# The last two output blocks of a diffusion layer: GpSimd's additions move to VectorE, ScalarE's products are added in one wide operation

## The chip, the cores and the metric

The kernel runs on one core of a Trainium2 chip. A core has engines with their own instruction queues: TensorE (PE, matmuls; weight loads are shown as PEld), VectorE (DVE), ScalarE (ACT) and GpSimd (POOL) for arithmetic, and SyncE (SP), which here only issues transfers. Transfers between the main memory and the on-chip memory SBUF are also issued from ScalarE's and GpSimd's queues; all run on the same 16 DMA engines. TensorE writes its results to PSUM, which GpSimd does not read in this program. Engines meet through semaphores only.

The metric is the device time of one execution in microseconds (us).

## What is computed

One layer of a hybrid diffusion backbone on 384 tokens (128 context tokens, 256 latent tokens) of width 2048, all in float32. What matters here is the end of the layer, the second half of the feed-forward part:

```
ff = (silu(h @ w_ffn_gate) * (h @ w_ffn_up)) @ w_ffn_down
x  = x + ga2 * rmsnorm(ff, norm_post_ffn)
```

with

```
rmsnorm(x, g) = x * rsqrt(mean(x * x, axis=-1) + 1e-6) * g
```

`ga2` is a gate for each channel, one for context and one for latent tokens. The output is `x`, transposed: channels on the 128 partitions, tokens along the row.

## The kernel before

The kernel holds activations transposed (16 blocks of 128 channels by 384 tokens) and streams all weights from the main memory. Each weight is split into a high and a low part, and each product is made of three matmuls of the parts. That fills nearly all of the time; the change stands behind it, in the last 15 us, where the down projection of the last hidden chunk ends and the result is normalised, gated, added to `x` and stored. The order of instructions there is the order in which the code issues them, on all five engines (`manual_schedule`, L1897): no scheduler moves anything, and only waits delay it.

The 384 tokens are three tiles `t` of 128 (tile 0 context, tiles 1 and 2 latent). For each tile the sum over chunks lies in SBUF with tokens on partitions, as four units `unit(t, n)` of 512 channels (L1551). For a tile the end goes:

- `last_products` (L1911): TensorE's last matmuls into the banks `pdn`. `add_last` (L1820): VectorE adds a bank to its unit, ScalarE sums the squares.
- `most`, `factor`, `inverse` (L1921 to L1932): the factor `r = 1 / sqrt(mean + eps)` of each token.
- `scale` (L1934): a unit times `r`, on VectorE or ScalarE, 512 wide.
- `turn` (L1944): TensorE transposes four 128x128 pieces of a unit into a PSUM tile `py[t, q]`. Where the unit isn't scaled, it multiplies by `dg` instead of the identity: `dg` is the identity times `r` (L2011), so that transposing and scaling are one matmul.
- `final(t, k)` (L1955): the gate `mods[:, 5, k]` (with the norm's weight folded in) times the piece, plus `x`, into `x1b`, which holds `x` and then the output. Either VectorE does both in one operation out of PSUM (L1964), or ScalarE makes the product into a scratch tile `ep` (L1961) and GpSimd adds it (L1962). `finals(t, q, on_act)` does the four pieces of unit `q`.
- `store` (L1966): one transfer of four pieces, 256 KB, from SyncE's queue or, where named, ScalarE's.

In tile 0 and tile 1 unit 1 goes over ScalarE and GpSimd. At the very end also unit 3 of tile 1 and unit 3 of tile 2 do:

```
finals(1, 3, True)
for q in (0, 1, 3, 2):
    turn(2, q, dg if q in (0, 2) else None)
store(12, 16, 1, 2)
finals(2, 3, True)
```

So GpSimd makes 16 additions of 128x128 here, four for each of these units, and two of the last five stores wait for it. After the last store every engine runs into the closing line of the program (L2093; L2097 in the changed kernel): SyncE waits for all output transfers, each engine drains, and all meet.

Of the kernel before, what the change touches and what calls it, by code (L numbers as in the profile page):

```python
# [20 lines left out]
P = 128  # L21
# [86 lines left out]
def tile_step(ctx: ExitStack, tc: tile.TileContext, a, o):  # L108
    nc = tc.nc
    PE, ACT, DVE, POOL, SP = nc.tensor, nc.scalar, nc.vector, nc.gpsimd, nc.sync  # L110
# [21 lines left out]
    mods = const.tile([P, 6, KT, 2], F32, name="mods")  # L132
# [886 lines left out]
    with ExitStack() as s:  # L1019
# [64 lines left out]
        for kb in range(0, KT, 4):  # L1084
            for x_ in range(2):
                for k in range(kb, kb + 4):
                    q = 32 * (k % 4)
# [9 lines left out]
    with ExitStack() as s:  # L1097
# [166 lines left out]
        for b, i in mix_order:  # L1264
# [18 lines left out]
            else:  # L1283
# [10 lines left out]
                p = psm.tile([P, T], F32, tag="mm", name="pmm")  # L1294
# [19 lines left out]
    with ExitStack() as s:  # L1314
# [5 lines left out]
        ep = [pe.tile([P, 512], F32, name=f"ep{n}", bufs=1) for n in range(6)]  # L1320
# [43 lines left out]
        for i in range(KT):  # L1364
            p = psm.tile([P, T], F32, tag="mm", name="pmm")
# [185 lines left out]
        def unit(t, n):  # L1551

            return psums[n // 2][:, 3 * (n % 2) + t, :]
# [192 lines left out]
        for u in range(HEAD):  # L1746
            kind, c, j = ffn_order[u]
            dst_of[kind](hp[u], c, j)
        n = 0
        for kind, c, j in ffn_order[HEAD:]:  # L1750
            p = psm.tile([P, T], F32, tag="mm", name="pmm")
# [82 lines left out]
        pd_tiles, hid_last, x1b, done = None, None, None, 0  # L1834
        for kind, c, i in steps[:-4]:
            last_c = c == NFC - 1 and kind == "D"
            if last_c and hid_last is not None and x1b is None:
                while pend:
                    pend.pop(0)()
                x1b = actp.tile([P, KT, T], F32, tag="A_hi", name="x1b")  # L1840
# [77 lines left out]
        def col(x, t):  # L1918
            return x[:, t : t + 1]
# [14 lines left out]
        def scale(eng, t, n):  # L1934
            f = unit(t, n)
            if eng is ACT:
                ACT.mul(f, f, col(r3, t))
            else:
                eng.tensor_scalar_mul(f, f, col(r3, t))

        py = {}
        py_pools = {0: [pss] * 4, 1: [psm] * 3 + [pss], 2: [pss] * 4}

        def turn(t, q, diag=None):  # L1944

            pool = py_pools[t][q]
            py[t, q] = pool.tile([P, 4, P], F32, tag="side" if pool is pss else "mm", name="py")
            for j in range(4):
                src = unit(t, q)[:, j * P : (j + 1) * P]
                if diag is None:  # L1950
                    PE.transpose(py[t, q][:, j, :], src, ident)
                else:
                    PE.matmul(py[t, q][:, j, :], src, diag, start=True, stop=True)

        def final(t, k, on_act=False):  # L1955

            src, dst = py[t, k // 4][:, k % 4, :], x1b[:, k, t * P : (t + 1) * P]
            m = mods[:, 5, k, min(t, 1) : min(t, 1) + 1]
            if on_act:
                tmp = ep[1 + k % 5][:, t * P : (t + 1) * P]  # L1960
                ACT.mul(tmp, src, m)  # L1961
                POOL.tensor_add(dst, dst, tmp)  # L1962
            else:
                DVE.scalar_tensor_tensor(dst, src, m, dst, op0=ALU.mult, op1=ALU.add)  # L1964

        def store(k0, k1, t0, t1, eng=SP):  # L1966
            cs = slice(t0 * P, t1 * P)
            eng.dma_start(o["yT"][:, k0:k1, cs], x1b[:, k0:k1, cs])
# [9 lines left out]
        def finals(t, q, on_act=False):  # L1978
            for k in range(4 * q, 4 * q + 4):
                final(t, k, on_act)  # L1980
# [29 lines left out]
        inverse(2)  # L2010
        DVE.tensor_scalar_mul(dg, ident, col(r3, 2))  # L2011
        scale(ACT, 2, 3)
        scale(DVE, 2, 1)
        finals(1, 3, True)
        for q in (0, 1, 3, 2):
            turn(2, q, dg if q in (0, 2) else None)
        store(12, 16, 1, 2)
        finals(2, 3, True)
        finals(2, 0)
        store(0, 4, 2, 3)  # L2020
        finals(2, 1)
        store(4, 8, 2, 3)
        finals(2, 2)
        store(12, 16, 2, 3)
        store(8, 12, 2, 3, ACT)

# [1 line left out]
def _tiles(w, n=P):  # L2028
# [74 lines left out]
```

## Time and profile before

| what | value |
|---|---|
| time, median of 3 runs | 1940.2 us (1939.46 to 1941.09) |
| span of the profiled execution, first to last instruction | 1937.5 us |
| TensorE busy | 1916.2 us (99%) |
| VectorE busy | 1650.8 us (85%) |
| ScalarE busy | 915.3 us (47%) |
| GpSimd busy | 85.8 us (4%) |
| additions of `final` on GpSimd (L1962) | 16, 456 ns each |

The profile is of one execution; what it gives of that execution's length is the span alone. "Busy" leaves out what the sequencers do by themselves (waits, drains, issuing transfers). In the groups of instructions a row reads: line, engine, operation, written tile <- read tiles, partitions x elements, count, then busy time, the mean of one, the idle time before them and who ended it. In the timeline a row begins with start and length in us, and instructions of one line that follow each other are merged.

### The profile page before, as it was taken

How to read it: one execution, taken by the hardware profiler on the slowest of the kernel's cores; microseconds unless marked ns; L12 is line 12 of the kernel's file. 1: busy time of each engine (PE TensorE's matmuls, PEld its weight loads, DVE VectorE, ACT ScalarE, POOL GpSimd, SP SyncE). 2: the span in 40 equal slices, each digit the busy share in tenths (PEclk: the TensorE clock that was granted, in tenths of full speed). 3: DMA queues.
4: the chain of work that ended last, by engine and by line, in shares of the span. 5: the costliest groups of instructions: out<-in, count | busy, mean ns of one | idle time of the engine just before them, and what ended most of it. 6: DMA issues, size and time to landing. Idle time of an engine off the chain costs nothing.

```text
span 1937.5 us, 27470 instructions
## 1 busy us (share of the span) xinstructions
PE 1916.2 (99%) x10494; PEld 1689.0 (87%) x10494; DVE 1650.8 (85%) x2168; ACT 915.3 (47%) x1301; POOL 85.8 (4%) x154
## 2 busy tenths in 40 slices
PE   8999999999999999999999999999999999999997
PEld 5679999999999999999988888888888888888886
DVE  5559897889969898978789888999998999988885
ACT  4235455545456654456454444444444443444444
POOL 0001111100000000104000000000000000000001
PEclk9999999999999999999999999999999999999999
DMA  9976766766757886655263636362636272625243
GB/s 389 392 280 229 259 232 224 255 227 198 223 170 244 303 287 208 233 196 196 89 198 126 199 107 196 115 214 95 218 102 217 88 223 92 201 76 185 87 174 110
DMA packets 200904, 380.53 MB, mean 196 GB/s; under 512 B 14228, under 2 KB 126964, under 8 KB 196420
## 3 DMA queue, kind: packets, MB, share of 16 engines
q1 hardware_dynamic: 181540, 320.84, 48.8%
q0 software_dynamic: 13952, 50.39, 8.4%
q10 hardware_dynamic: 5280, 7.55, 1.1%
q8 instruction: 82, 1.34, 0.3%
q14 instruction: 50, 0.41, 0.1%
HBM read 361.94 MB, written 16.78 MB: 195 GB/s over the span
## 4 chain that ended last, share of the span: by engine, by line
PE 92%; DMA 3%; DVE 3%; ACT 1%; issue 0%; SPq 0%; DVEq 0%; ACTq 0%
PE pgu L338 31%; PE pmm L326 31%; PE pdn L338 18%; PE pv L491 3%; DMA slab<-in_w_ada 2%; PE pfo L1043 1%; PE pf L1243 1%; PE pgm L474 1%; PE pmm L1520 1%; PE ptr L1812 1%; PE pfo L1044 1%; PE pf L1244 1%; PE po L788 1%; DVE wlo L287 0%; DMA raw<-in_w_br_gla 0%
## 5 line engine op out<-in xcount | busy, mean ns | idle before, releaser
L326 PE MATMUL pmm<-A_hi,whi 128*128 128x384 f32 x1088 | 366.9, 337 | 0.0
L326 PE MATMUL pmm<-A_lo,whi 128*128 128x384 f32 x1088 | 364.1, 335 | 0.3 <-DVE A_lo L379 0.3
L326 PE MATMUL pmm<-A_hi,wlo 128*128 128x384 f32 x1088 | 364.2, 335 | 0.0
L1667 ACT CAST whi<-u 128x1024 fp32r<-128x1024 f32 x200 | 210.7, 1053 | 271.9 <-DVE u L1651 86.2
L1667 ACT CAST whi<-raw 128x1024 fp32r<-128x1024 f32 x175 | 184.1, 1052 | 211.9 <-DMA raw<-in_w_g 73.6
L1678 DVE TENSOR_TENSOR wlo<-u,whi 128x1024 fp32r<-128x1024 f32 x200 | 244.2, 1221 | 28.0 <-ACT whi L1667 16.8
L338 PE MATMUL pgu<-whi,A_hi 128*128 128x512 f32 x640 | 250.0, 391 | 0.0
L338 PE MATMUL pgu<-whi,A_lo 128*128 128x512 f32 x640 | 249.3, 389 | 0.0
L1678 DVE TENSOR_TENSOR wlo<-raw,whi 128x1024 fp32r<-128x1024 f32 x175 | 213.5, 1220 | 34.2 <-ACT whi L1667 24.6
L287 DVE TENSOR_TENSOR wlo<-raw,whi 128x1024 fp32r<-128x1024 f32 x165 | 200.8, 1220 | 32.4 <-ACT whi L300 32.1
L300 ACT CAST whi<-raw 128x1024 fp32r<-128x1024 f32 x151 | 158.0, 1049 | 125.5 <-DMA raw<-in_w_out 46.5
L707 DVE SCALAR_TENSOR_TENSOR adacc<-adaw,spad,adacc 128x1024 f32<-128x1024 f32 x170 | 210.4, 1279 | 3.3 <-DMA adaw<-in_w_ada 3.1
L326 PEld LDWEIGHTS pmm<-A_hi,whi 128*128 128x128 f32 x1088 | 204.2, 188 | 3.3 <-issue 1.7
L326 PEld LDWEIGHTS pmm<-A_lo,whi 128*128 128x128 f32 x1088 | 204.4, 188 | 1.0 <-DVE A_lo L379 0.8
L326 PEld LDWEIGHTS pmm<-A_hi,wlo 128*128 128x128 f32 x1088 | 204.2, 188 | 0.4 <-DVE wlo L287 0.2
L338 PE MATMUL pdn<-whi,hid_hi 128*128 128x512 f32 x480 | 186.9, 389 | 0.0
L338 PE MATMUL pdn<-whi,hid_lo 128*128 128x512 f32 x480 | 186.8, 389 | 0.0
L338 PE MATMUL pgu<-wlo,A_hi 128*128 128x512 f32 x640 | 184.2, 389 | 0.0
L338 PEld LDWEIGHTS pgu<-whi,A_hi 128*128 128x128 f32 x640 | 120.1, 188 | 26.1 <-issue 0.8
L338 PEld LDWEIGHTS pgu<-wlo,A_hi 128*128 128x128 f32 x640 | 120.1, 188 | 25.4
L338 PEld LDWEIGHTS pgu<-whi,A_lo 128*128 128x128 f32 x640 | 120.1, 188 | 25.0
L338 PE MATMUL pgu<-whi,S 128*128 128x512 f32 x480 | 131.1, 395 | 0.0
(398 smaller groups left out, 2998.4 us busy)
## 6 DMA issues: line engine op xcount, KB each, us to landing
adaw<-in_w_ada POOLq DMA_DIRECT2D x96, 512.0 KB, 3.9
raw<-in_w_d SPq DMA_DIRECT2D x88, 512.0 KB, 4.0
slab<-in_w_ada SPq DMA_DIRECT2D x32, 1024.0 KB, 10.3
raw<-in_w_gate SPq DMA_DIRECT2D x64, 512.0 KB, 4.3
raw<-in_w_g SPq DMA_DIRECT2D x48, 512.0 KB, 3.8
raw<-in_w_u SPq DMA_DIRECT2D x48, 512.0 KB, 3.8
raw<-in_w_in SPq DMA_DIRECT2D x46, 512.0 KB, 4.5
u<-in_w_u SPq DMA_DIRECT2D x40, 512.0 KB, 4.6
```

Of the source, the lines that this page charges most:

```text
L287: eng.tensor_sub(lo, raw, hi.bitcast(F32))
L300: ACT.copy(hi, raw)
L326: PE.matmul(dst, w[wi][:, k * n + n0 : k * n + n0 + P], x[xi][:, k0 + k, :], start=first and k == 0 and j == 0, stop=last and k == kts - 1 ...
L338: PE.matmul(dst, stat[x_][m], mov(w[w_], m), start=first and w_ == m == x_ == 0, stop=last and w_ == m == 1,)
L474: PE.matmul(pgv[q : q + 32, :], spad[:, k, :], slab[k // (KT // 2)][:, k % (KT // 2), :], start=k < 4, stop=k >= KT - 4,)
L491: PE.matmul(pv[2 * t + g], hT[x_][:, kb, t * P : (t + 1) * P], w_[:, g * 512 : (g + 1) * 512], start=kb == 0 and j == 0, stop=kb == KT - 1 ...
L707: DVE.scalar_tensor_tensor(acc[:, c, :], w, spad[:, k, c : c + 1], acc[:, c, :], op0=ALU.mult, op1=ALU.add,)
L788: PE.matmul(dst, w[wi], x[xi], start=first and j == 0, stop=last and j == 2)
L1043: PE.matmul(p, w_of[0][:, i, k, g, :], x[:, :, lo:hi], start=kt == 0, stop=False)
L1044: PE.matmul(p[:, 0], w_of[1][:, i, k, g, :], x[:, 0, lo:hi], start=False, stop=kt == KT - 1)
L1667: ACT.copy(hi, src)
L1678: DVE.tensor_sub(lo, src, hi.bitcast(F32))
```

## The change

GpSimd's additions for unit 3 of tile 1 and unit 3 of tile 2 go. Unit 3 of tile 1 takes the way over VectorE alone. Unit 1 of tile 2 is scaled by ScalarE instead of VectorE. TensorE transposes unit 3 of tile 2 ahead of units 1 and 2. ScalarE still makes the four products of that unit, but into the four quarters of one scratch tile `ep[4]`, and VectorE adds that tile to `x1b` in one operation of 128x4x128, between the blocks of units 1 and 2. The store of that unit moves from SyncE's queue to ScalarE's, and that of unit 2, now the last, to SyncE's.

```diff
         inverse(2)
         DVE.tensor_scalar_mul(dg, ident, col(r3, 2))
         scale(ACT, 2, 3)
-        scale(DVE, 2, 1)
-        finals(1, 3, True)
-        for q in (0, 1, 3, 2):
+        scale(ACT, 2, 1)
+        finals(1, 3)
+        for q in (0, 3, 1, 2):
             turn(2, q, dg if q in (0, 2) else None)
         store(12, 16, 1, 2)
-        finals(2, 3, True)
+        wide = ep[4].rearrange("p (j x) -> p j x", j=4)
+        for k in range(12, 16):
+            ACT.mul(wide[:, k - 12, :], py[2, 3][:, k - 12, :], mods[:, 5, k, 1:2])
         finals(2, 0)
         store(0, 4, 2, 3)
         finals(2, 1)
         store(4, 8, 2, 3)
+        last = x1b[:, 12:16, 2 * P : 3 * P]
+        DVE.tensor_add(last, last, wide)
+        store(12, 16, 2, 3, ACT)
         finals(2, 2)
-        store(12, 16, 2, 3)
-        store(8, 12, 2, 3, ACT)
+        store(8, 12, 2, 3)
```

GpSimd's queue, its last rows. `x1b` is the output tile, `ep` the scratch tiles with ScalarE's products (the numbers tell them apart). Before:

```order
L1962 TENSOR_TENSOR x1b<-x1b,ep_7649 128x128
L1962 TENSOR_TENSOR x1b<-x1b,ep_7651 128x128
L1962 TENSOR_TENSOR x1b<-x1b,ep_7647 128x128
L1962 TENSOR_TENSOR x1b<-x1b,ep_7648 128x128
L1962 TENSOR_TENSOR x1b<-x1b,ep_7649 128x128 x2
L1962 TENSOR_TENSOR x1b<-x1b,ep_7650 128x128
L1962 TENSOR_TENSOR x1b<-x1b,ep_7651 128x128
L1962 TENSOR_TENSOR x1b<-x1b,ep_7647 128x128
L1962 TENSOR_TENSOR x1b<-x1b,ep_7649 128x128
L1962 TENSOR_TENSOR x1b<-x1b,ep_7650 128x128
L1962 TENSOR_TENSOR x1b<-x1b,ep_7651 128x128
L1962 TENSOR_TENSOR x1b<-x1b,ep_7647 128x128
```

and now:

```order
L1962 TENSOR_TENSOR x1b<-x1b,ep_7649 128x128
L1962 TENSOR_TENSOR x1b<-x1b,ep_7651 128x128
L1962 TENSOR_TENSOR x1b<-x1b,ep_7647 128x128
L1962 TENSOR_TENSOR x1b<-x1b,ep_7648 128x128
L1962 TENSOR_TENSOR x1b<-x1b,ep_7649 128x128
L2097 UNCONDITIONAL_BRANCH
```

Both begin with the last addition of tile 0; the four behind it are unit 1 of tile 1 (before, the row with x2 holds its last one and the first of the next unit). The eight of the two last units are gone, and the branch to the closing line follows at once.

VectorE's queue from tile 2's factor on (`r` the factor, L2011 the scaled identity `dg`, `psums` the units, L1964 the blocks of `final`, `py` the transposed units), the difference of the two:

```order
 L1932 RECIPROCAL r_9635<-r_9635 128x1
 L2011 TENSOR_SCALAR ep_7646<-ident,r_9635 128x128
-L1939 TENSOR_SCALAR psums<-psums,r_9635 128x512
 L1964 SCALAR_TENSOR_TENSOR x1b<-py,mods,x1b 128x128 x12
-L2093 UNCONDITIONAL_BRANCH
+L2026 TENSOR_TENSOR x1b<-x1b,ep_7650 128x4x128
+L1964 SCALAR_TENSOR_TENSOR x1b<-py,mods,x1b 128x128 x4
+L2097 UNCONDITIONAL_BRANCH
```

The scaling is gone. The twelve operations of L1964 were units 0, 1 and 2 of tile 2; now the first four of them are unit 3 of tile 1, and the wide addition (L2026) stands ahead of the last four.

ScalarE's queue in the same place (L1929 is tile 2's factor, L1937 the scaling of a unit, L1961 and L2020 the products, L1968 the store). Before:

```order
L1929 ACTIVATE r_9635<-ssq,bias_16826 128x1
L1937 ACTIVATE psums<-psums,r_9635 128x512
L1961 ACTIVATE ep_7649<-py,mods 128x128
L1961 ACTIVATE ep_7650<-py,mods 128x128
L1961 ACTIVATE ep_7651<-py,mods 128x128
L1961 ACTIVATE ep_7647<-py,mods 128x128
```

and now:

```order
L1929 ACTIVATE r_9635<-ssq,bias_16826 128x1
L1937 ACTIVATE psums<-psums,r_9635 128x512 x2
L2020 ACTIVATE ep_7650<-py,mods 128x128 x4
L1968 DMA out_yT<-x1b 128x4x128
L2097 UNCONDITIONAL_BRANCH
```

The four products shown before are those of unit 3 of tile 1; they are gone and a second scaling stands in their place. The four products of unit 3 of tile 2 all go to one tile now, and the store behind them is that of unit 3 instead of unit 2.

## The prediction

> **What bounds the kernel now.** I read the page first, then the chain of waits at its end.
>
> ```profile
> span 1937.5 us, 27470 instructions
> ...
> PE 92%; DMA 3%; DVE 3%; ACT 1%; issue 0%; SPq 0%; DVEq 0%; ACTq 0%
> ```
>
> ```profile
> 1923.82 0.30 DVE ep L2011
> 1924.11 0.14 issue
> 1924.25 1.14 PE py L1953 x8
> ...
> 1927.58 1.03 DVE x1b L1964 x4
> ```
>
> TensorE carries 92% of the chain, and the change touches none of that: only the last 14 us can move. The second fence is that end (start, duration, what). The chain view stops at VectorE's last operation, 1927.58 + 1.03 = 1928.61, yet the span runs to 1937.5. The missing 8.9 us hold only sequencer work, so I asked for the rows of the kernel's closing line, L2093 (the end of the program), and of its opening, L2085 (durations min/median/max in ns, then first and last start).
>
> ```profile
> L2093 POOLq DRAIN  x3: 46/102/9207, 1927.5 to 1937.2; - x3
> L2093 SPq DRAIN  x3: 7/7/7, 1932.7 to 1936.9; - x3
> ...
> L2093 DVEq DRAIN  x2: 19/739/1459, 1927.2 to 1937.0; - x2
> L2093 ACTq DRAIN  x2: 8/80/153, 1929.1 to 1936.9; - x2
> ```
>
> ```profile
> L2085 POOLq DRAIN  x1: 182/182/182, 0.3 to 0.3; - x1
> ```
>
> ```profile
> SPq L2093 <- PEq L2093: 4.5, 2, 4.1
> SPq L2093 <- DMA out_yT<-x1b: 3.3, 4, 1.2
> ```
>
> Each engine ends in a DRAIN, which is over when the engine is empty, and then all meet. GpSimd's first one starts at 1927.5 and takes 9.207 us, to 1936.7; the closing exchange brings the span to 1937.5, so that exchange is 0.8 us. Everyone else is done much earlier: SyncE, which waits for the output transfers, drains at 1932.7 and then idles 4.1 us (third fence: us in all, times, longest; the engine named there, PE, has long been done, and the only work still open is GpSimd's). So the end is **set by GpSimd's drain**, 4 us behind the last transfer.
>
> ```profile
> 1921.19 1.70 POOL L1962 TENSOR_TENSOR x1b<-x1b,ep 128x128 f32<-128x128 f32 x4 [2.24 <-ACT ep L1961]
> 1924.87 1.69 POOL L1962 TENSOR_TENSOR x1b<-x1b,ep 128x128 f32<-128x128 f32 x4 [1.99 <-ACT ep L1961]
> 1926.73 1.69 POOL L1962 TENSOR_TENSOR x1b<-x1b,ep 128x128 f32<-128x128 f32 x4 [0.17 <-ACT ep L1961]
> ```
>
> GpSimd's last addition ends at 1926.73 + 1.69 = 1928.42, so the drain lasts 8.3 us beyond it. VectorE's drain ends 0.05 us after its last operation (1927.2 + 1.459 = 1928.66), ScalarE's takes 0.15 us: only GpSimd's outlasts its work.
>
> The Trainium skill, "Perfetto Trace Analysis", section "Per-engine timelines", says that of a sequencer-only instruction such as DRAIN the profiler reports the execution alone, and the wait for semaphores lies before it. By that the 9.207 us are GpSimd's own work; were they a wait for the transfers, the gain would be that of the second rival below.
>
> ```profile
> L691 POOL DMA_DIRECT2D adaw<-in_w_ada x96 | 51.0, 531 | 751.9 <-DVE adacc L707 457.1 <-DVE vr L379 132.5 <-DVE adacc L705 78.8
> ...
> L1012 POOL DMA_DIRECT2D wr<-in_w_br_four x4 | 2.3, 582 | 0.3 <-POOL wr L1007 0.3
> ```
>
> One thing sets this drain apart from the 0.182 us one at the start: between them GpSimd issued 100 transfers. Neither kernel differs there, so I take 8.3 us behind the last addition as a constant.
>
> **The other end: the transfers.** All output goes out in stores of 256 KB.
>
> ```profile
> 1926.59 2.29 SPq L1968 DMA_DIRECT2D out_yT<-x1b  x4
> ...
> 1928.64 0.40 ACTq L1968 DMA_DIRECT2D out_yT<-x1b  x1
> ```
>
> ```profile
> out_yT<-x1b SPq DMA_DIRECT2D x1, 256.0 KB, 2.3
> ```
>
> ```profile
> out_yT<-x1b ACTq DMA_DIRECT2D x1, 256.0 KB, 4.0
> ```
>
> ```profile
> 1928.00:1930.00 2.00, 0.00 (x0) 0.00 (x0) 0.61 (x3) 0.00 (x0) 0.42 (x2) 0.79 1.01 281
> 1930.00:1932.00 2.00, 0.00 (x0) 0.00 (x0) 0.00 (x0) 0.00 (x0) 0.00 (x0) 0.50 0.99 291
> ...
> 1933.00:1936.00 3.00, 0.00 (x0) 0.00 (x0) 0.00 (x0) 0.00 (x0) 0.00 (x0) 0.50 0.00 0
> ```
>
> The first store of all, on an idle queue, landed after 2.3 us (second fence); the last, ScalarE's, after 4.0, at 1928.64 + 4.0 = 1932.6. The windows (last columns: granted clock, DMA share, GB/s) show why: the engines are full at 291 GB/s, and 262144 B / 291 GB/s = 0.90 us a store. Five stores go out from 1926.59: 1926.59 + 2.3 + 4 x 0.90 = 1932.5. They are a queue, not a latency. SyncE's first drain follows that landing by 0.1 us (1932.7), and for its last bookkeeping I allow 0.2 in all; nothing moves from 1933 on, only the drain runs.
>
> **The change, part by part.** *GpSimd* loses its last eight additions, two of the three groups above. Its last one then ends at 1921.19 + 1.70 = 1922.89, and the drain at 1922.89 + 8.3 = 1931.2. Nothing waits for those eight but two of SyncE's stores.
>
> *VectorE, second tile.* Out goes the scaling of unit 1 (L1939), in come four operations of L1964.
>
> ```profile
> 1924.02 0.48 DVE L1939 TENSOR_SCALAR psums<-psums,r 128x512 f32<-128x512 f32 x1
> 1925.42 0.35 DVE L1964 SCALAR_TENSOR_TENSOR x1b<-py,mods,x1b 128x128 f32<-128x128 f32 x1 [0.92 <-PE py L1953]
> ```
>
> ```profile
> 1927.49 1.12 DVE L1964 SCALAR_TENSOR_TENSOR x1b<-py,mods,x1b 128x128 f32<-128x128 f32 x4
> ```
>
> Four of these take 1.12 us, so they run from 1924.02 to 1925.14. VectorE stood there anyway: 0.48 us of scaling and 0.92 us waiting for TensorE, until 1925.42. The cover is 0.28 us; without it the last operation would come later by what is missing. Cost 0. The store of that block is issued at about 1925.2 instead of 1926.59.
>
> *ScalarE and TensorE.*
>
> ```profile
> 1923.82 0.72 ACT L1937 ACTIVATE psums<-psums,r 128x512 f32<-128x512 f32 x1 [0.23 <-DVE r L1932]
> 1924.44 1.12 ACT L1961 ACTIVATE ep<-py,mods 128x128 f32<-128x128 f32 x4
> 1926.29 1.14 ACT L1961 ACTIVATE ep<-py,mods 128x128 f32<-128x128 f32 x4 [0.72 <-PE py L1951]
> ```
>
> ```profile
> 1925.22 1.04 PE L1951 MATMUL py<-ident,psums 128*128 128x128 f32 x8
> ```
>
> ScalarE loses four products at 1924.44 and puts its second scaling there, done at 1924.44 + 0.72 = 1925.16. TensorE's plain transposes start at 1925.22, now unit 3 (scaled by 1924.54) before unit 1, so neither waits. Unit 3 is half of the 1.04 us, out at 1925.8; ScalarE's four products then take 1.14 us, to 1927.0.
>
> *VectorE, third tile.* The wide addition (128x4x128, both inputs in SBUF) stands behind the blocks of units 0 and 1, at 1927.49; the products are there 0.5 us before. Behind it queues the last block, unit 2.
>
> ```profile
> L1796 DVE TENSOR_TENSOR ep<-ep,ep x10: 691/691/693, 995.3 to 1844.7; 128x512 f32<-128x512 f32 x10
> ```
>
> ```profile
> 1901.67 1.89 DVE L1822 TENSOR_TENSOR psums<-psums,pdn 128x512 f32<-128x512 f32 x3 [0.99 <-PE pdn L338]
> 1906.80 0.68 DVE L1822 TENSOR_TENSOR psums<-psums,pdn 128x512 f32<-128x512 f32 x1
> ```
>
> An addition of this size takes 0.69 us; in a row the next starts (1.89 - 0.68) / 2 = 0.61 us on. VectorE ends at 1928.61 + 0.61 = 1929.22. The stride of x1b isn't in these rows: I bound the operation by 0.61 and twice that.
>
> The Trainium skill, "SBUF — State Buffer", section "SBUF: two separate sides", speaks against such an addition: a VectorE operation with two SBUF inputs and a GpSimd operation that reads SBUF exclude each other for their whole length. GpSimd's additions are over by 1922.89; only if the drain counted as such an operation would the time be the third rival's.
>
> *Stores.* Now one at 1925.2, then 1926.6, 1927.6, 1928.2 (ScalarE's, which waits for the wide addition with nothing queued behind it) and 1929.25. With 2.3 us alone and 0.90 us behind another: 1927.5; 1928.9; 1929.9; 1930.8; 1931.7. The last one is issued 0.6 us later than before and lands 0.9 us earlier, because one store went out of the queue ahead of it.
>
> **Sum.** SyncE is through at 1931.7 + 0.2 = 1931.9, GpSimd at 1931.2. The later sets the end: 1931.9 + 0.8 = 1932.7, against 1937.5: **-4.8 us**. The drain goes from 4 us behind the transfers to 0.7 us ahead, so a further gain there would be worth nothing. Bounds: the last store at best 1929.25 + 2.3 = 1931.55, end 1932.55, -4.95 us; at worst the 4.0 us of the row above, end 1934.25, -3.25 us, or with the addition at twice its price -2.65. I take the queue's value, since it gives the 1932.6 of before within 0.1. The profile gives only the span of its execution; the median of the timed runs, 1940.2, is 2.7 us more, which I carry over: 1932.7 + 2.7 = **1935.4**.
>
> **Rivals.** *First, a stretched drain:* beside VectorE and the transfers it takes longer than alone. It has 0.7 us to spare; at 12 us behind the last addition the end is 1922.9 + 12 + 0.8 = 1935.7, time 1938.4. Against: half of the old one ran beside full transfers.
>
> *Second, the drain doesn't follow the additions,* but the last landing, 4.1 us behind it (1936.7 - 1932.6), or it is that long only under the profiler. Then what counts is the 0.9 us of the landing: 1939.3. For: GpSimd's last addition, VectorE's last operation and the drain's start lie within 1.2 us here, so the trace can't separate them, and the timed runs carry no trace. Against: the drain's row begins 5 us before that landing.
>
> *Third, a shared lock:* the drain holds the wide addition until 1931.2, 3.7 us late; VectorE ends 1932.9, the last store lands 1935.2, end 1936.2, time 1938.9. For: no VectorE operation with two SBUF inputs runs during the old drain. Against: a drain reads no tensor.
>
> *Fourth, on the other side:* the drain makes progress only once VectorE is still. The last VectorE operation at 1928.61 and GpSimd's last at 1928.42 lie 0.2 us apart, so the 8 us could as well count from VectorE. Then GpSimd's early finish is worth nothing and VectorE's 0.61 us are lost: 1929.2 + 8.3 + 0.8 = 1938.3, time 1941.0. It decides as soon as VectorE's end comes later than 1928.6. Against: GpSimd's additions keep their pace beside VectorE's (1.70 and 1.69 us for four).
>
> **Chances.** Forecast 0.76, stretched drain 0.05, second 0.10, third 0.03, fourth 0.06. 0.2% is 3.9 us, about what a measurement of this kernel can tell from no change. The forecast's own range is 1934.4 to 1937.5, and 0.05 of its 0.76 gain less than 3.9 us. Faster by over 0.2%: 0.71 plus 0.03 of the stretched drain, 0.74. Slower by over 0.2%: the fourth reaches only +0.8 us, and I leave 0.03 above it. Within: 0.23. The range must hold 0.8: forecast and stretched drain do, so it ends at 1938.4; below, -4.95 us and 0.7 us for the spread of the runs (1939.46 to 1941.09) give 1934.4.
>
> **What would show it.** GpSimd's long drain starting near 1921.9 and ending near 1931.2; SyncE's last wait in L2093 down from 4.1 us to some tenths; VectorE's last operation ending at 1929.2; the wide addition at 0.69 us; the last landing near 1931.7. Wrong if the drain still ends after 1932 (stretched, second or fourth, told apart by its start and by what ends just ahead of it), or if VectorE waits at the wide addition (third).

## The result, and the profile after

| | before | after |
|---|---|---|
| time, median of 8 runs each | 1940.35 us (1939.17 to 1941.09) | 1934.99 us (1934.49 to 1936.06) |
| ratio after / before, with its 95% interval | | 0.9975 (0.9966 to 0.9983) |
| span of the profiled execution | 1937.5 us | 1933.4 us |
| first matmul of L1953 to the end of the span | 13.22 us | 8.49 us |

The changed kernel is faster: by its interval 3.3 to 6.6 us, by the medians 5.4. The forecast was 1935.4. The last row of the table is the best ruler for the two traces: L1953's first matmul is the first step on TensorE after tile 2's factor, and everything that was edited stands behind it or beside it. Its 4.74 us are not blurred by what one execution loses earlier.

The page of the changed kernel, its first line and the chain by engine:

```profile
span 1933.4 us, 27462 instructions
...
PE 93%; DVE 3%; DMA 3%; ACT 1%; issue 1%; SPq 0%; DVEq 0%; ACTq 0%
```

The chain is the same as before up to the last microseconds. Here is its end (start, duration, what):

```profile
1924.92 1.14 PE py L1953 x8
...
1927.99 0.26 DVEq L2097
1928.25 0.60 DVE x1b L2026
1928.85 1.04 DVE x1b L1964 x4
```

L1953 starts at 1924.92; before it was 1924.25. This execution is 0.67 us late there, so each time that the prediction gave must be read with 0.67 us added. The lateness is no part of the change: 0.11 us of it stands at 1885 us, 0.56 us come between 1886 and 1888, and up to L1953 nothing more is added. The end of the span, to two decimals, is 1933.41 - 1924.92 = 8.49 us behind L1953.

Now the closing line, L2097, the row that carried the old end first (durations min/median/max in ns, first and last start):

```profile
L2097 POOLq DRAIN  x3: 46/102/9235, 1922.6 to 1933.1; - x3
L2097 SPq DRAIN  x3: 7/7/7, 1932.6 to 1932.9; - x3
...
L2097 DVEq DRAIN  x2: 19/1042/2064, 1927.9 to 1932.9; - x2
L2097 ACTq DRAIN  x2: 8/80/152, 1929.3 to 1932.9; - x2
```

GpSimd's drain is as long as before (9.235 us, then 9.207), but begins at 1922.6 and is over at 1931.8. SyncE's first drain comes at 1932.6, so the drain now ends 0.7 us **ahead** of the transfers, where it ended 4 us behind them. SyncE's waits say the same (us in all, times, longest; PE, which is named in the second row, is only the last to be seen in the meeting of all engines):

```profile
SPq L2097 <- DMA out_yT<-x1b: 1.7, 2, 0.8
SPq L2097 <- PEq L2097: 0.7, 2, 0.5
```

The row counts two waits. Before, they took 4.1 us, for GpSimd's drain, and some 0.5 us in the closing exchange (4.5 in all). Now the first takes 0.2 us; the 0.5 us is the closing exchange, which has not changed. The end in the timeline (start, length, engine, line):

```profile
1921.86 1.71 POOL L1962 TENSOR_TENSOR x1b<-x1b,ep 128x128 f32<-128x128 f32 x4 [2.23 <-ACT ep L1961]
...
1924.69 1.12 DVE L1964 SCALAR_TENSOR_TENSOR x1b<-py,mods,x1b 128x128 f32<-128x128 f32 x4
...
1926.09 2.16 DVE L1964 SCALAR_TENSOR_TENSOR x1b<-py,mods,x1b 128x128 f32<-128x128 f32 x8 [0.28 <-PE py L1953]
1926.53 1.15 ACT L2020 ACTIVATE ep<-py,mods 128x128 f32<-128x128 f32 x4 [0.70 <-PE py L1951]
...
1928.17 0.68 DVE L2026 TENSOR_TENSOR x1b<-x1b,ep 128x512 f32<-128x512 f32 x1
1928.77 1.12 DVE L1964 SCALAR_TENSOR_TENSOR x1b<-py,mods,x1b 128x128 f32<-128x128 f32 x4
1928.88 0.40 ACTq L1968 DMA_DIRECT2D out_yT<-x1b  x1
```

GpSimd's last addition ends at 1921.86 + 1.71 = 1923.57; the drain lasts 8.26 us beyond it, as before. VectorE's last operation ends at 1928.77 + 1.12 = 1929.89, and the stores land 2.5 to 2.7 us after their issue (KB, median us to landing):

```profile
out_yT<-x1b SPq DMA_DIRECT2D x5, 256.0 KB, 2.5
out_yT<-x1b ACTq DMA_DIRECT2D x1, 256.0 KB, 2.7
```

### The profile page after: what moved, and what is told of

It is laid out like the page before. It is cut to its first block, busy times and chain, and to the rows that moved or that the text cites. A ratio compares the mean times of both kernels' runs of the same rounds, so it can differ in the third digit from the quotient of the medians.

```text
span 1933.4 us, 27462 instructions
## 1 busy us (share of the span) xinstructions
PE 1916.9 (99%) x10494; PEld 1689.6 (87%) x10494; DVE 1652.2 (85%) x2172; ACT 915.8 (47%) x1298; POOL 82.7 (4%) x146
## 4 chain that ended last, share of the span: by engine, by line
PE 93%; DVE 3%; DMA 3%; ACT 1%; issue 1%; SPq 0%; DVEq 0%; ACTq 0%
PE pmm L326 31%; PE pgu L338 31%; PE pdn L338 18%; PE pv L491 3%; DMA slab<-in_w_ada 2%; PE pfo L1043 1%; PE pgm L474 1%; PE pf L1243 1%; PE pmm L1520 1%; PE ptr L1812 1%; PE pfo L1044 1%; PE pf L1244 1%; PE po L788 1%; DVE wlo L287 0%; DMA raw<-in_w_d 0%
```

## The experiments

Two readings had to be told apart. The **constant-drain theory** is that of the prediction: GpSimd's closing drain takes some 8.3 us behind its last operation, whatever else runs, and set the old end. The **transfers-only theory** is its second rival: the drain follows the last landing, or is that long only under the profiler, and the gain comes from the stores. Behind them stood a second question, why this drain is so long at all. Each kernel was timed against the kernel before on the same chip; "beyond" means the time from the end of GpSimd's last operation to the end of its drain, from the two instructions in the trace.

**A late operation on GpSimd.** The changed kernel with one addition on GpSimd, which nothing waits for:

```diff
             ACT.mul(wide[:, k - 12, :], py[2, 3][:, k - 12, :], mods[:, 5, k, 1:2])
+        POOL.tensor_add(ep[3][:, 0:P], ep[3][:, 0:P], wide[:, 3, :])
         finals(2, 0)
```

> The changed kernel plus one GpSimd addition of 128x128 that waits for ScalarE's last product and that nobody reads. Constant-drain theory (GpSimd's drain ends 8.26 us after its last operation, in timed runs as in the profile, and the program ends 0.75 us after the later of that drain and SyncE's): the operation ends near 1928.1 in the changed kernel's own time, the drain near 1936.4, span 1937.1 against 1933.4, time 1935.0 + 3.7 = 1938.7 us, ratio to the kernel before 0.9992. Transfers-only theory (the long drain exists only under the profiler, and the gain comes from the stores): the profile shows the late drain, but the time stays at 1935.0 us, ratio 0.9972.

Time 1939.16 us against 1940.11, ratio 0.9994 (0.9985 to 1.0003): a small operation that is on nobody's path takes back nearly the whole gain. The closing line and GpSimd's last row:

```profile
L2098 POOLq DRAIN  x3: 46/102/8740, 1926.9 to 1936.2; - x3
L2098 SPq DRAIN  x3: 7/7/7, 1931.7 to 1935.9; - x3
```

```profile
1926.96 0.45 POOL L2021 TENSOR_TENSOR ep<-ep,ep 128x128 f32<-128x128 f32 x1 [4.25 <-ACT ep L2020]
```

The operation ends at 1927.41 and the drain at 1926.94 + 8.74 = 1935.68, 8.26 us beyond. SyncE is through with the transfers (its first drain) at 1931.7, 3.9 us earlier. The drain follows GpSimd's last operation and not the landing, and the timed runs, which carry no trace, show its price too. The transfers-only theory falls.

**Only one of the two units moved.** Unit 3 of tile 1 stays on ScalarE and GpSimd, the rest is the changed kernel:

```diff
-        scale(ACT, 2, 1)
-        finals(1, 3)
+        scale(DVE, 2, 1)
+        finals(1, 3, True)
...
-        wide = ep[4].rearrange("p (j x) -> p j x", j=4)
+        wide = ep[2].rearrange("p (j x) -> p j x", j=4)
```

> Only the half of the change for tile 2: GpSimd keeps unit 3 of tile 1 (and VectorE scales unit 1 of tile 2), while unit 3 of tile 2 is added by VectorE in one wide operation. Constant-drain theory: in the time of the kernel before GpSimd's last addition ends at 1926.6 instead of 1928.4, the drain at 1934.8, span 1935.6 against 1937.5, time 1940.35 - 1.85 = 1938.5 us, ratio 0.9990. Transfers-only theory: five stores from 1926.6 as before, last landing 1932.5 as before, time 1940.3 us, ratio 1.0000.

Time 1938.44 us, ratio 0.9989 (0.9981 to 0.9998), as expected.

```profile
L2097 POOLq DRAIN  x3: 46/102/9220, 1926.7 to 1936.4; - x3
L2097 SPq DRAIN  x3: 7/7/7, 1933.8 to 1936.2; - x3
```

```profile
1925.95 1.70 POOL L1962 TENSOR_TENSOR x1b<-x1b,ep 128x128 f32<-128x128 f32 x4 [1.99 <-ACT ep L1961]
```

The last addition ends at 1927.65, the drain at 1935.91: 8.26 us beyond again, and 2.1 us behind SyncE. The end is 11.4 us behind L1953, against 13.2 before and 8.5 with the whole change. So moving the last unit alone takes 1.9 us off, and the other unit the remaining 2.9, until the transfers are last.

**Half of GpSimd's transfers, and none.** Both on the kernel before, whose additions stay; only the queue that issues the adaLN weights at L691 changes (the second one also moves the four transfers of L1012):

```diff
-                POOL.dma_start(w, a["w_ada"][m - 2, half, k])
+                (SP if k % 2 else POOL).dma_start(w, a["w_ada"][m - 2, half, k])
```

```diff
-                POOL.dma_start(w, a["w_ada"][m - 2, half, k])
+                SP.dma_start(w, a["w_ada"][m - 2, half, k])
...
-    nyq_load(POOL, 0)
+    nyq_load(SP, 0)
```

> The kernel before, with 48 of GpSimd's 100 transfers issued from SyncE's queue instead. What makes the drain long? If it passes over the transfers that GpSimd has issued: 8.26 x 52/100 = 4.3 us behind the last addition, and the program ends with the last store, span about 1933.6 plus whatever SyncE's fuller queue costs earlier. If one issued transfer is enough: 8.26 us. If it has nothing to do with them: 8.26 us.

> The kernel before, with all 100 of GpSimd's transfers issued from SyncE's queue. If the drain's length comes from them, by number or by there being any: about 0.1 us behind the last addition, as the 0.18 us drain at the program's start, and the span ends with the last store, about 1933.6 plus whatever SyncE's fuller queue costs earlier (it may cost much: SyncE then waits for VectorE between weight loads). If not: 8.26 us.

The closing line and GpSimd's last additions with half of them:

```profile
L2093 POOLq DRAIN  x3: 46/102/5292, 1928.8 to 1934.6; - x3
L2093 SPq DRAIN  x3: 7/7/7, 1934.0 to 1934.3; - x3
```

```profile
1928.02 1.69 POOL L1962 TENSOR_TENSOR x1b<-x1b,ep 128x128 f32<-128x128 f32 x4 [0.17 <-ACT ep L1961]
```

and with none:

```profile
L2093 POOLq DRAIN  x3: 34/77/1012, 1930.8 to 1936.8; - x3
```

```profile
1930.10 1.69 POOL L1962 TENSOR_TENSOR x1b<-x1b,ep 128x128 f32<-128x128 f32 x4 [0.16 <-ACT ep L1961]
```

Beyond the last addition the drain lasts 4.34 us with 52 transfers and 0.07 us with none. The length of the drain comes from the transfers that GpSimd issued, although the last of them went out at 824 us, more than a millisecond earlier. Times: 1937.30 us, ratio 0.9985 (0.9976 to 0.9994), and 1937.38, 0.9986 (0.9976 to 0.9995). In these traces, half first, L1953 starts later than in the kernel before:

```profile
1925.53 1.13 PE L1953 MATMUL py<-ep,psums 128*128 128x128 f32 x8 [1.82 <-DVE ep L2011]
```

```profile
1927.62 1.13 PE L1953 MATMUL py<-ep,psums 128*128 128x128 f32 x8 [1.83 <-DVE ep L2011]
```

In these executions 1.3 and 3.4 us are lost ahead of the end. Behind L1953 the span lasts 9.3 and 9.4 us, 3.9 and 3.8 less than before; by the medians the kernels are only 2.8 and 2.7 us faster, so moving transfers off GpSimd's queue isn't free here. So of the 4.74 us that the change takes off the end, 3.8 to 3.9 are the drain that is no longer last, and the remaining 0.9 us are the transfers: SyncE is through 7.65 us behind L1953 in the changed kernel, 8.50 us in the kernel before.

**No additions on GpSimd at the end.** The changed kernel, where VectorE also does unit 1 of tiles 0 and 1; GpSimd is through after some 900 us:

```diff
-            finals(0, q, q == 1)
+            finals(0, q)
...
-            finals(1, q, q == 1)
+            finals(1, q)
```

> The changed kernel without any GpSimd addition at the end: unit 1 of tiles 0 and 1 goes over VectorE too. If the drain counts for nothing once it is hidden: it starts as soon as GpSimd's last earlier work is done, hundreds of us before the end, lasts 8.2 us there as well (100 transfers x 0.082 us), and the end is that of the stores; VectorE has 8 x 0.26 = 2.1 us more to do, of which 1 to 2 us stand in front of the last block: time 1936 to 1937 us, slower than the changed kernel. If an earlier drain still saves something: up to 0.8 us faster than the changed kernel, 1934.2 us.

Time 1938.64 us, ratio 0.9991 (0.9982 to 1.0000): slower than the changed kernel, and by more than expected.

```profile
L2097 POOLq DRAIN  x3: 46/102/11800, 894.5 to 1936.6; - x3
```

```profile
895.69 2.40 POOL L287 TENSOR_TENSOR wlo<-raw,whi 128x1024 fp32r<-128x1024 f32 x1
```

```profile
1921.93 2.16 DVE L1964 SCALAR_TENSOR_TENSOR x1b<-py,mods,x1b 128x128 f32<-128x128 f32 x8
...
1924.52 0.68 DVE L1822 TENSOR_TENSOR psums<-psums,pdn 128x512 f32<-128x512 f32 x1
...
1927.01 1.85 PE L1953 MATMUL py<-ep,psums 128*128 128x128 f32 x8 [3.70 <-DVE ep L2011]
...
1928.65 1.91 PE L1951 MATMUL py<-ident,psums 128*128 128x128 f32 x8
```

The drain ran at 898 us, where every other engine is at work, and again 8.26 us beyond the last operation (895.69 + 2.40 = 898.09, end 906.35). It is a constant in the middle of the program as well. The time went elsewhere. First, VectorE now has eight blocks (2.16 us) ahead of its last sum of tile 2 (L1822), on which tile 2's factor rests: L1953 starts at 1927.01, 2.1 us later than in the changed kernel. Second, the end grew from 8.5 to 9.9 us behind L1953, because the eight transposes take 1.85 and 1.91 us instead of 1.13 and 1.04. The windows show why; of this kernel first, of the changed kernel below it (the last three columns: granted clock, DMA share, GB/s):

```profile
1926.00:1928.00 2.00, 0.99 (x5) 1.02 (x6) 1.72 (x7) 1.65 (x4) 0.00 (x0) 0.81 0.39 118
1928.00:1930.00 2.00, 2.00 (x12) 2.00 (x11) 1.10 (x4) 0.25 (x1) 0.00 (x0) 0.50 0.49 145
```

```profile
1926.00:1928.00 2.00, 1.82 (x17) 1.63 (x15) 1.91 (x8) 1.15 (x4) 0.00 (x0) 1.00 0.62 186
```

TensorE's clock fell to a half after it had idled for 3.70 us, and by the trace stayed there for 3.4 us; the changed kernel idles for 1.83 us in the same place and keeps 1.00. The Trainium skill, "TensorE: Matmul & The Clock Gate", section "HAM oscillation — how this bites in real kernels", warns of gaps of more than about 3.4 us, and the two traces agree with it (3.70 us: half the clock, 1.83 us: none lost). A third trace, of the run with 96 halves out of 100 further down, shows it in the middle of the program. The first row is the matmul behind a gap of 3.72 us, the second a window just after it, with the clock at 0.50:

```profile
748.00 0.45 PE L326 MATMUL pmm<-A_lo,whi 128*128 128x384 f32 x1 [3.72 <-DVE A_lo L379]
```

```profile
749.50:752.50 3.00, 3.00 (x11) 3.00 (x10) 2.00 (x2) 2.97 (x7) 0.00 (x0) 0.50 0.00 0
```

A shorter gap isn't safe for that: at the end of the kernel before, TensorE's last matmul ends at 1927.15, and the mean clock of 0.79 between 1928 and 1930, which the prediction shows, puts the fall from 1.00 to 0.50 at 1929.2, only 2.0 us later. What such a gap would cost isn't shown, since no matmul follows it.

**Half stores at the end.** The changed kernel, each of SyncE's three stores of tile 2 cut into two of 128 KB, the first issued after two blocks; shown for the last one:

```diff
-        finals(2, 2)
-        store(8, 12, 2, 3)
+        for k in range(8, 12):
+            final(2, k)
+            if k % 2:
+                store(k - 1, k + 1, 2, 3)
```

> The changed kernel with six of tile 2's stores halved (two pieces, 128 KB), each issued as soon as its two pieces are there; ScalarE's store stays whole. If the queue of stores from the first block of tile 2 on sets the end now: it starts 0.5 us earlier, the last half store is issued at the same moment and lands 1.9 instead of 2.5 us later, so the part of the span from TensorE's last scaled transposes (L1953) to the end falls from 8.45 us to about 8.0, where the drain stops it; the time by 0.4 us, which is less than these rounds tell. If a store's fixed latency sets it: the last landing and the end stay as they are within 0.1 us.

Time 1935.30 us, ratio 0.9976 (0.9966 to 0.9986). From L1953 (1925.01) to the end it takes 8.5 us, so nothing is gained, and the expected 0.45 us were wrong.

```profile
out_yT<-x1b SPq DMA_DIRECT2D x6, 128.0 KB, 2.0
```

```profile
SPq L2100 <- DMA out_yT<-x1b: 1.7, 2, 1.3
SPq L2100 <- PEq L2100: 0.7, 2, 0.5
```

With half the bytes a store lands after 2.0 us, the last one after 2.2 us, so most of a store's 2.5 us does not depend on its size. The last landing came only 0.29 us earlier behind L1953 (1932.23 - 1925.01 = 7.22, against 1932.43 - 1924.92 = 7.51). The rest went in SyncE: it waits for ten semaphores of the stores one after another in a fixed order, and the one that came last stood fourth, with six more behind it that take 0.06 us each; in the changed kernel it stood ninth. SyncE's drain followed the last landing by 0.45 us instead of 0.14.

**What in the transfers counts.** Five kernels that differ from the kernel before only at L691, in how many transfers GpSimd issues and how many rows each has. All 96 in two halves of 64 rows:

```diff
-                POOL.dma_start(w, a["w_ada"][m - 2, half, k])
+                for z in range(2):
+                    POOL.dma_start(w[64 * z : 64 * z + 64, :], a["w_ada"][m - 2, half, k][64 * z : 64 * z + 64, :])
```

> The kernel before, with each of GpSimd's 96 transfers of 512 KB made as two of 64 partitions each: same bytes, same rows, 196 transfers instead of 100. If the drain goes by the number of transfers issued: 196 x 0.082 = 16.1 us behind the last addition, the span 7.9 us longer, time 1948 us. If by bytes or rows moved: 8.26 us, time 1940 us.

Time 1942.28 us, ratio 1.0012 (1.0002 to 1.0022). Neither number came out:

```profile
L2094 POOLq DRAIN  x3: 46/102/7165, 1931.9 to 1939.6; - x3
```

```profile
1931.13 1.69 POOL L1963 TENSOR_TENSOR x1b<-x1b,ep 128x128 f32<-128x128 f32 x4 [0.17 <-ACT ep L1962]
```

6.22 us beyond, less than with 100 transfers. Two readings were left: a half transfer costs less, or part of the 196 had been cleared before the end. The next kernels tell them apart: GpSimd issues one half of each and SyncE the other; and every second one, three of sixteen, four of sixteen in halves on GpSimd, with the same loop as above.

```diff
+                for z, e in enumerate((POOL, SP)):
+                    e.dma_start(w[64 * z : 64 * z + 64, :], a["w_ada"][m - 2, half, k][64 * z : 64 * z + 64, :])
```

```diff
+                n = 64 if k % 2 else 128
+                for z in range(0, 128, n):
+                    POOL.dma_start(w[z : z + n, :], a["w_ada"][m - 2, half, k][z : z + n, :])
```

(`k in (1, 6, 11)` in place of `k % 2` for 118, `k in (1, 5, 9, 13)` for 124.)

> The kernel before, where GpSimd issues the first 64 rows of each of the 96 adaLN weight transfers and SyncE the other 64: GpSimd issues 100 transfers as before, 96 of them of half the rows. In the run with 196 transfers, 192 of them halves, the drain lasted 6.2 us beyond the last addition. Number theory (0.082 us for each transfer still on the books, whatever its rows; some of the 196 were cleared earlier): 8.26 us beyond the last addition again. Rows theory (a half transfer costs less; by that run (6.15 - 0.35) / 192 = 0.030 us, with 0.35 us for the four others): 0.35 + 96 x 0.030 = 3.3 us.

> The kernel before, where every second of the 96 transfers is issued in two halves of 64 rows: 48 whole, 96 half and 4 others, 148 on GpSimd. Rows theory: 0.35 + 48 x 0.082 + 96 x 0.030 = 7.2 us beyond the last addition. Number theory without a limit: 148 x 0.082 = 12.2 us; with a clearing on the way, as the 6.2 us for 196 would need (196 - 75 = 121 cleared), less: 148 - 121 = 27, 2.3 us, if 121 are cleared at once as soon as some number between 100 and 148 is reached.

> The kernel before, where three of every sixteen adaLN weight transfers are issued in two halves of 64 rows: 118 transfers on GpSimd. Number theory with 121 cleared at once when the books are full (100 issued left 100; 148 left 27, 196 left 75, both 121 fewer): nothing is cleared yet, the drain lasts 0.07 + 118 x 0.082 = 9.7 us beyond the last addition. A gradual clearing, or one at fewer than 118: less than 8.3 us.

> The same with four of every sixteen transfers in halves: 124 on GpSimd, 6 more than the run with 118. Number theory with 121 cleared at once: if the clearing comes by the 124th, 3 are left, 0.07 + 3 x 0.082 = 0.3 us beyond the last addition. If it comes only later (between 124 and 148): 0.07 + 124 x 0.082 = 10.2 us. A gradual clearing: between the two.

The drains of the four, in this order, each with the row of the last additions:

```profile
L2094 POOLq DRAIN  x3: 46/102/9202, 1942.7 to 1952.4; - x3
```

```profile
1941.98 1.69 POOL L1963 TENSOR_TENSOR x1b<-x1b,ep 128x128 f32<-128x128 f32 x4 [0.16 <-ACT ep L1962]
```

```profile
L2095 POOLq DRAIN  x3: 46/102/3248, 1930.8 to 1936.6; - x3
```

```profile
1930.05 1.69 POOL L1964 TENSOR_TENSOR x1b<-x1b,ep 128x128 f32<-128x128 f32 x4 [0.17 <-ACT ep L1963]
```

```profile
L2095 POOLq DRAIN  x3: 46/102/10680, 1929.3 to 1940.5; - x3
```

```profile
1928.53 1.69 POOL L1964 TENSOR_TENSOR x1b<-x1b,ep 128x128 f32<-128x128 f32 x4 [0.17 <-ACT ep L1963]
```

```profile
L2095 POOLq DRAIN  x3: 46/102/11167, 1929.4 to 1941.0; - x3
```

```profile
1928.62 1.69 POOL L1964 TENSOR_TENSOR x1b<-x1b,ep 128x128 f32<-128x128 f32 x4 [0.17 <-ACT ep L1963]
```

All of them in one table (the last column is the beyond less the 0.07 us of no transfers, over 0.082 us):

| transfers GpSimd issued | of them halves | last operation ends | drain ends | beyond | transfers' worth |
|---|---|---|---|---|---|
| 0 | 0 | 1931.79 | 1931.86 | 0.07 us | 0 |
| 52 | 0 | 1929.71 | 1934.05 | 4.34 us | 52 |
| 100 (kernel before) | 0 | 1928.42 | 1936.68 | 8.26 us | 100 |
| 100 | 96 | 1943.67 | 1951.93 | 8.26 us | 100 |
| 118 | 36 | 1930.22 | 1939.95 | 9.73 us | 118 |
| 124 | 48 | 1930.31 | 1940.53 | 10.22 us | 124 |
| 148 | 96 | 1931.74 | 1934.04 | 2.30 us | 27 |
| 196 | 192 | 1932.81 | 1939.03 | 6.22 us | 75 |

The price goes by the number of transfers and not by their rows: 96 halves cost what 96 whole ones do. It is 0.082 us for each up to 124 (10.15 us / 124). With 148 and with 196 the same 121 are missing from the drain (148 - 27, 196 - 75). The simplest reading is that 121 are cleared at once, somewhere behind the 124th and at the latest with the 148th. No instruction of the two traces is longer by the 10 us that this should take, so where and when it is done stays open. The kernels with 96 halves out of 100, with 118, 124 and 148 ran once each (1954.49, 1942.51, 1943.12 and 1938.71 us, the kernel before 1940.16 to 1940.48 beside them). That the first is 14 us slower was not pursued: in its trace 13.7 us are lost before 851 us, far ahead of the end, and behind L1953 it takes 13.2 us, as the kernel before does.

**The changed kernel once more.**

> The changed kernel once more beside these, without an edit: 1935.0 us, ratio to the kernel before 0.9973, and the drain again 8.26 us behind the last addition.

Time 1935.34 us (1934.49 to 1937.08, 11 runs) against 1940.13 in the second set of runs, ratio 0.9976 (0.9966 to 0.9985). Its trace repeats the first one's end:

```profile
L2097 POOLq DRAIN  x3: 46/102/9223, 1923.2 to 1933.8; - x3
L2097 SPq DRAIN  x3: 7/7/7, 1933.2 to 1933.5; - x3
```

The drain is over at 1932.42, 0.8 us ahead of SyncE.

## Why the prediction was right, step by step

**What bounded the kernel.** "The end is set by GpSimd's drain, 4 us behind the last transfer": shown, twice over. Moving the drain back by one stray addition costs nearly what the change gained, and taking its transfers away from the kernel before, additions left in place, takes 3.8 to 3.9 us off its end.

**GpSimd.** The drain as a constant of 8.3 us: 8.258 before, 8.261 after, 8.26 in every kernel with 100 transfers, at 898 us as at 1927. Its end was put at 1931.2, with the 0.67 us 1931.87; measured 1931.83. The prediction tied the constant to the 100 transfers on the strength of one comparison with the drain at the start. That was a guess, which the sum didn't need, since neither kernel changes them; the runs with 0 to 124 transfers show that it was right.

**VectorE, tile 2.** Cost 0 with a cover of 0.28 us: the four blocks ran from 1924.69 to 1925.81 and VectorE then waited 0.28 us for TensorE.

**ScalarE and TensorE.** Products done at 1927.0, so 1927.67: measured 1926.53 + 1.15 = 1927.68.

**The wide addition.** 0.69 us, 0.61 to the next: measured 0.68 and 0.60. The stride of `x1b`, bounded by twice the price, cost nothing. VectorE's end at 1929.22, so 1929.89: measured 1929.89.

**Stores.** ScalarE's landing at 1930.8 and the last at 1931.7, so 1931.47 and 1932.37: measured 1931.55 and 1932.43. Between the two lie 0.88 us, the 0.90 of a queue that is full. The last one landed 2.5 us after its issue, against 2.3 alone, so here the queue adds only 0.2 us.

**The sum.** -4.8 us: at the end of the two traces -4.74. The span itself differs by 4.1, since the traced execution was 0.67 us late ahead of the end, and the medians by 5.4 and, in the second set, 4.8. That the median came within 0.4 us of the forecast is in part luck, since two errors offset each other: the span was put 0.7 us too short (1932.7, measured 1933.4), and the 2.7 us carried over from span to median were only 1.6 (1934.99 - 1933.4). The lower end of the range was also added up wrongly: 1940.2 - 4.95 - 0.7 is 1934.55 and not 1934.4. The median lies above both. The reserve of 0.7 us between drain and transfers is there as well (0.74).

**The rivals.** The stretched drain: 8.26 us beside VectorE, transfers and all, so no. The drain that follows the landing or the profiler: refuted by the late operation. The shared lock: the wide addition started at 1928.17 while the drain ran (to 1931.83), waited for nothing and took its 0.68 us. The Trainium skill, "SBUF — State Buffer", section "SBUF: two separate sides", has a VectorE operation with two SBUF inputs exclude a GpSimd operation that reads SBUF, and by these rows the drain doesn't act as one. The drain that counts from VectorE: it ended 1.9 us behind VectorE's last operation, not 8.3.

**The split.** The prediction had both parts: the drain 4 us behind the transfers, and a last landing 0.9 us earlier. The runs without or with half of GpSimd's transfers measure them apart, as 3.8 to 3.9 and 0.9 us. It also said that a further gain at the drain would be worth nothing; what nothing in it said is that going further, with no addition on GpSimd at all, loses 3.3 us (1938.64 against 1935.34 in the same set).

## What to carry to other kernels

Look at the closing line of the program: if one engine's DRAIN ends behind the last landing, everything behind that engine's last operation is on the path, however idle the engine looks, and the cure is to end its work early or to issue its transfers elsewhere. Count the transfers that GpSimd's queue issues before giving GpSimd work near the end. And stop once the drain lies ahead of the transfers: what it frees beyond that is worth nothing, while the work still has to fit on an engine that is on the path.

## What the runs showed of the hardware

GpSimd's closing drain costs 0.082 us for each transfer that was issued from its queue, long ago or not, of 64 or of 128 rows (0.07 us for none, 10.22 for 124). The cost grows with the number only up to some point between 124 and 148; beyond it 121 are missing, and 148 transfers cost 2.30 us. Each number of transfers was traced once, except 100. GpSimd's last additions keep their length (1.69 to 1.71 us for four), though the drain's row opens before they end, and VectorE's operations beside the drain keep theirs (0.68 us for the wide addition, 1.12 us for four blocks). Gaps of 3.70 and 3.72 us on TensorE halved its clock for some 3.4 us; the first cost 0.7 and 0.9 us for eight transposes.
